# An encoder layer on one core: first front in half blocks, weight buffers, maxima and residual

## The chip, the core and the metric

The kernel runs on one core of one Trainium2 chip. It is measured in device microseconds for one execution, from start to end. The engines are named as in the profile: PE is TensorE (matrix products; PEld is its loading of weights), DVE is VectorE, ACT is ScalarE, POOL is GpSimd, SP is SyncE, which here only issues DMAs. Each engine works through its own instructions in the order in which they were laid down; a DMA issue is an instruction of the engine that issues it.

## The reference

One layer on 512 tokens of 2048 numbers, in float32. A layer norm; a projection whose columns split into a convolution group and a matrix-memory group (mLSTM, 8 heads); a mixing product and a second norm; then PEER: each token picks 8 x 16 of 16384 single-neuron experts by product keys, and the layer ends in a third norm.

```
def reference(x, ln_in_g, ln_in_b, w_in, b_gate, conv_w, conv_b, mh_norm_g, w_out,
              ln1_g, ln1_b, peer_wq, peer_keys, peer_u, peer_v, ln2_g, ln2_b):
    h = layernorm(x, ln_in_g, ln_in_b)
    for l in range(DEPTH):
        proj = h @ w_in[l]
        cB, cC, ch, q, k, v, o, gi, gf = jnp.split(proj, split_at, axis=-1)
        y_conv = cB * causal_dwconv(cC * ch, conv_w[l], conv_b[l])
...
        hm = mlstm_chunkwise(hd(q), hd(k), hd(v), logi, logf)
        hm = layernorm(hm, mh_norm_g[l].reshape(M_HEADS, M_HEAD_DIM),
...
        y_m = jax.nn.sigmoid(o) * hm.reshape(Bn, S, D_MLSTM)
        mix = jnp.concatenate([y_conv, y_m], axis=-1) @ w_out[l]
        h = layernorm(ALPHA * h + mix, ln1_g[l], ln1_b[l])
        ff = peer_ffn(h, peer_wq[l], peer_keys[l], peer_u[l], peer_v[l])
        h = layernorm(ALPHA * h + ff, ln2_g[l], ln2_b[l])
    return h

def peer_ffn(h, wq, keys, u, v):
...
        q = (xt @ wq).reshape(-1, PEER_HEADS, 2, PEER_HALF)
        s = jnp.einsum('thpc,hpnc->thpn', q, keys)
        sv, si = lax.top_k(s, PEER_TOPK)
...
        ue = jnp.take(u, eid, axis=0)
        act = jax.nn.gelu(jnp.einsum('thkd,td->thk', ue, xt).astype(jnp.float32), approximate=False)
        ve = jnp.take(v, eid, axis=0)
        return jnp.einsum('thk,thkd->td', (gate * act).astype(xt.dtype), ve)
```

## The kernel before

All weights arrive as **chunks** of 1 MB, tiles `raw` of 128 x 2048 numbers, 432 of them in the program. `load_split` (L90) issues the load on SP, and `split` (L81) cuts the chunk into two parts for three-pass products: ACT writes `hi`, the rounded value (L86), DVE writes `lo`, what is left (L87). `mm3` (L97 to L100) then makes three matmuls for each product: hi by hi (L98), with one low part (L99), with the other (L100). Which operand is the weight differs by stage; in the first front `lo` is read by L99, later by L100. `raw` has three buffers in the pool `wp`, `hi` and `lo` two each. A new `hi` waits until PE has finished the chunk that had its buffer before, and a new load waits until DVE has written the `lo` of the chunk three before.

The program goes through five parts.

- **First front** (`rows_block`, L311): the first 128 tokens go through the whole layer up to the choice of their experts, so that fetching can start early. It reads 56 chunks of the input projection (with `heads0`, `conv0` and the norms of the later tokens, `ln_later`, between them), 16 of the mixing product and 16 of the PEER query. A chunk is 12 matmuls of 512 columns.
- **Projections** of the other 384 tokens: `v_half` (8 chunks), then `head(h)` and `conv_block` (48 chunks), run in turns, three yields each (L660). A chunk is 48 matmuls of 384 columns. `head` makes q, k and the output gate; loads the head's stabilising maxima, `bM` (L611, one buffer), on SP; makes the weights W from them on ACT (L626, L623) and DVE (L622, L624), and the score tiles PJ (L631). After the first yield come the numerators (L641) and on DVE the denominators and statistics (L643 to L649); after the second the normalised rows `hm` (L655), which PE transposes (L656).
- **Mixing** (L673): 16 chunks of `w_out`, 36 matmuls of 512 columns each. `mix_out` (L683) fetches a piece of the residual, `hr` (L686, one buffer, issued by ACT), and adds it on DVE (L687). Then the norm, transposes (`to_t`) and the first query chunks.
- **Selection** (L744): the other queries, the top-16 choices, 32 hidden chunks (`u_chunk`, L735), and the weights of the chosen experts, spread into tables on PE and DVE (`build`, L803; its matmuls are L821, its table `wg`), which are written to DRAM as `w_d`.
- **Last stage** (L873): hidden chunks and value chunks (`v_part`, L913) for 320 tokens, 48 matmuls of 320 columns each; `make_g` (L897) multiplies a hidden chunk by a piece `wt` of the table, read back from `w_d` (L893). `AHEAD + MORE` hidden chunks, 32 + 3, are made before the loop and kept in DRAM.

Beside all this the first 128 tokens and half of the next 128 get their experts by **fetched rows** (`gather`, L507): POOL fetches 128 rows into a tile `gt`, and DVE multiplies them (L519 for u, L532 for v). These jobs are handed out by `advance`: `RATE_PROJ` = 1.5 for each chunk of projections and mixing, `RATE_MID` = 0.8 for each of the 32 hidden chunks, and the rest evenly over the last stage. `gt` has two buffers until the last stage and three in it (`gpool2`), and `flush(len(turn_[0]) - 1)` puts the product of a row one fetch behind it, or two in the last stage.

The order on each engine is made by a scheduler when the program is built; `high_priority` around the split puts `hi` and `lo` ahead of other work.

Of the kernel before, what the change touches and what calls it, by code (L numbers as in the profile page):

```python
# [8 lines left out]
F32 = mybir.dt.float32  # L9
# [10 lines left out]
P = 128  # L20
# [18 lines left out]
MORE = 3  # L39
# [6 lines left out]
RATE_PROJ = 1.5  # L46
# [6 lines left out]
def tile_kernel(ctx: ExitStack, tc: tile.TileContext, x, lin_g, lin_b, w_rows, w_proj, w_v, w_gate, b_gate,  # L53
# [24 lines left out]
    def raw_tile():  # L78
        return wp.tile([P, 2048], F32, name="raw", bufs=3)

    def split(raw, hi=None, lo=None, prio=PRIO):  # L81
        with tc.high_priority(offset=prio):
            if hi is None:
                hi = wp.tile([P, 2048], F32R, name="hi")
                lo = wp.tile([P, 2048], F32R, name="lo")
            ACT.activation(hi, raw, AF.Copy)  # L86
            DVE.tensor_sub(lo, raw, hi.bitcast(F32))  # L87
        return hi, lo

    def load_split(src, hi=None, lo=None):  # L90
        raw = raw_tile()
        nc.sync.dma_start(raw, src)
        return split(raw, hi, lo)
# [35 lines left out]
    def stats_tile():  # L129
        return stat.tile([P, 4, 6], F32, name="st", bufs=6)  # L130
# [173 lines left out]
    f0 = ExitStack()  # L304
    fy = f0.enter_context(tc.tile_pool(name="fy", bufs=1))
# [5 lines left out]
    def rows_block(src, b, xT):  # L311
        ps = pacc.tile([P, S], F32, name="acc")
        for pc in range(4):
            w = load_split(src[b, pc])
            for k in range(4):
                kk = 4 * pc + k
                mm3(ps, [a[:, kk, :] for a in xT], [a[:, k * S:(k + 1) * S] for a in w], kk == 0, kk == KD - 1)
        return ps
# [174 lines left out]
    f0.close()  # L493


    gpools = [ctx.enter_context(tc.tile_pool(name="gpool", bufs=2, side="right"))]
    turn_ = ["AA"]
    count = [0]
# [8 lines left out]
    def gather(src, idx):  # L507
        gt = gpools["AB".index(turn_[0][count[0] % len(turn_[0])])].tile([P, D], F32, name="gt")
        count[0] += 1
        ins = nc.gpsimd.indirect_dma_start(out=gt, out_offset=None, in_=src,  # L510
                                           in_offset=bass.IndirectOffsetOnAxis(ap=idx, axis=0))
        if last_mm[0] is not None:
            tc.add_manual_dep(ins.ins, last_mm[0].ins.name, SCHED, reason="gathers keep pace with the products")
        return gt

    def slot_jobs(idx, gate, rows, n, scale):
        def u_slot(s):
# [3 lines left out]
            flush(len(turn_[0]) - 1)  # L521
# [6 lines left out]
        def v_slot(s):  # L528
# [4 lines left out]
            flush(0 if s == n - 1 else len(turn_[0]) - 1)  # L533
# [14 lines left out]
    with ExitStack() as p1:  # L548
# [50 lines left out]

        def head(h):  # L600
            pq = proj_chunk(w_proj[24 + h], hT)
# [8 lines left out]
            bM = w2.tile([P, NL], F32, name="bM", bufs=1)  # L610
            nc.sync.dma_start(bM, bass.AP(tensor=nM_d.tensor, offset=nM_d.offset + h * S + P, ap=[[0, P], [1, NL]]))  # L611
# [61 lines left out]
    with ExitStack() as p1b:  # L673
        big = p1b.enter_context(tc.tile_pool(name="big2", bufs=1))
        lnp = p1b.enter_context(tc.tile_pool(name="lnp2", bufs=1))
        w2 = p1b.enter_context(tc.tile_pool(name="w3", bufs=1))
# [3 lines left out]
        r = big.tile([P, LT, D], F32, name="r32")  # L680
        sts = [stats_tile() for _ in range(LT)]

        def mix_out(ps, t, db):  # L683
            ds_ = slice(db * S, (db + 1) * S)
            hr = w2.tile([P, S], F32, name="hr")
            nc.scalar.dma_start(hr, h_d[:, t, ds_])  # L686
            DVE.scalar_tensor_tensor(r[:, t, ds_], hr, ALPHA, ps, op0=OP.mult, op1=OP.add)  # L687
# [182 lines left out]
    gpools.append(ctx.enter_context(tc.tile_pool(name="gpool2", bufs=1, side="right")))  # L870
    turn_[0] = "AAB"

    with ExitStack() as p3:  # L873
        ap = p3.enter_context(tc.tile_pool(name="accp", bufs=1))
# [87 lines left out]
        for kind, n in order:  # L962
# [3 lines left out]
            else:  # L966
# [9 lines left out]
              else load_split(vb[124 + db]) for db in range(4)]  # L976
        accO = [gpools[0].tile([P, D], F32, name="gt"), gpools[0].tile([P, D], F32, name="gt"),
                gpools[1].tile([P, D], F32, name="gt")]
# [107 lines left out]
```

## Time and profile before

| | before |
|---|---|
| time, median of 3 runs (lowest to highest) | 3341.19 us (3338.57 to 3356.52) |
| time of the profiled execution | 3352.37 us |
| its span | 3350.6 us |
| PE busy | 3095.6 us, 92% |
| DVE busy | 2779.4 us, 83% |
| ACT busy | 1149.2 us, 34% |
| DMA traffic | 947.44 MB, mean 283 GB/s |
| mean granted PE clock | 0.967 |

The profiled execution lies 11.2 us above the median of the runs. A share of busy time is a mean over parts with different limits, so the rows below are read part by part. The first front lasts until about 400 us, the projections until 1012, mixing until 1215, the selection until 1720 and the last stage from there to the end. Times in rows are counted from the start of the span.

### The profile page before, as it was taken

To read this page: it belongs to the slowest core of one execution; us is meant where nothing else is said; L and a number is where in the kernel's file an instruction comes from. 1 tells how busy PE (TensorE), PEld (TensorE's weight loads), DVE (VectorE), ACT (ScalarE), POOL (GpSimd) and SP (SyncE) were. 2 spreads that over 40 slices of the span, in tenths; PEclk is the share of its full clock that TensorE was granted. 3 is DMA by queue.
4 is the path that set the end of the run, shared out by engine and by line. 5 is a ranking of instruction groups with operands and counts; after the bars stand their busy time and mean duration, and the time that the engine had idled before them with its cause. 6 is when DMAs were issued, how large, how long until landed. Compare 5 with 4: busy or idle time off the path is not lost. (4 is left out here: it accounts for less than half of the span.)

```text
span 3350.6 us, 46462 instructions
## 1 busy us (share of the span) xinstructions
PE 3095.6 (92%) x19047; PEld 2931.8 (87%) x19047; DVE 2779.4 (83%) x3835; ACT 1149.2 (34%) x1107; POOL 670.4 (20%) x400
## 2 busy tenths in 40 slices
PE   6886888888988899999969999999999999999997
PEld 4665668888987699999969999999999999999995
DVE  7876877676767769998859999898889888889888
ACT  5554423332332223333323333333333333333332
POOL 0000012212222100110102122323223322333222
PEclk9999999999999989999979999999999999999999
DMA  7787557666767623666659999999999999899983
GB/s 274 284 300 259 212 220 258 253 241 241 266 247 289 258 104 121 234 251 239 245 192 354 359 351 345 338 350 344 339 352 338 344 345 351 328 348 343 348 318 130
DMA packets 183383, 947.44 MB, mean 283 GB/s; under 512 B 16818, under 2 KB 70850, under 8 KB 74434
## 3 DMA queue, kind: packets, MB, share of 16 engines
q1 hardware_dynamic: 116000, 496.52, 41.0%
q0 software_dynamic: 55296, 402.68, 32.1%
q10 hardware_dynamic: 11874, 45.28, 3.6%
q8 instruction: 149, 2.44, 0.3%
q14 instruction: 64, 0.52, 0.0%
HBM read 906.61 MB, written 37.21 MB: 282 GB/s over the span
## 5 line engine op out<-in xcount | busy, mean ns | idle before, releaser
L86 ACT ACTIVATE hi<-raw 128x2048 fp32r<-128x2048 f32 x427 | 818.1, 1916 | 1447.5 <-PE ph L99 594.7
L87 DVE TENSOR_TENSOR lo<-raw,hi 128x2048 fp32r<-128x2048 f32 x427 | 976.1, 2287 | 123.5 <-ACT hi L86 117.1
L100 PE MATMUL ph<-tth,lo 128*128 128x320 f32 (+3 forms) x2336 | 733.1, 314 | 5.1 <-DVE lo L87 5.1
L98 PE MATMUL ph<-tth,hi 128*128 128x320 f32 (+3 forms) x2336 | 732.9, 314 | 3.9 <-ACT gl L741 3.9
L99 PE MATMUL ph<-ttl,hi 128*128 128x320 f32 (+3 forms) x2336 | 733.8, 314 | 0.0
L98 PE MATMUL po<-gh,hi 128*128 128x320 f32 x1984 | 612.7, 309 | 21.0 <-ACT gh L909 18.3
L99 PE MATMUL po<-glo,hi 128*128 128x320 f32 x1984 | 613.1, 309 | 3.3 <-DVE glo L910 3.2
L100 PE MATMUL po<-gh,lo 128*128 128x320 f32 x1984 | 612.7, 309 | 3.5 <-DVE lo L87 3.5
L510 POOL DMA_INDIRECT gt<-in_u_dram,idx x192 | 319.0, 1661 | 1331.4 <-PE ph L99 419.9
L519 DVE SCALAR_TENSOR_TENSOR gt<-gt,rows 128x2048 f32<-128x2048 f32 x192 | 439.1, 2288 | 148.9 <-DMA gt<-in_u_dram,idx 148.5
L510 POOL DMA_INDIRECT gt<-in_v_dram,idx x192 | 328.7, 1712 | 795.7 <-PE po L99 278.6
L532 DVE SCALAR_TENSOR_TENSOR rows<-gt,wts,rows 128x2048 f32<-128x2048 f32 x192 | 450.6, 2347 | 27.5 <-DMA gt<-in_v_dram,idx 27.1
L100 PEld LDWEIGHTS ph<-tth,lo 128*128 128x128 f32 x2336 | 444.6, 190 | 6.9 <-DVE lo L87 6.9
L98 PEld LDWEIGHTS ph<-tth,hi 128*128 128x128 f32 x2336 | 444.6, 190 | 4.5 <-ACT gl L741 4.1
L99 PEld LDWEIGHTS ph<-ttl,hi 128*128 128x128 f32 x2336 | 444.6, 190 | 0.0
L98 PEld LDWEIGHTS po<-gh,hi 128*128 128x128 f32 x1984 | 372.4, 188 | 22.6 <-ACT gh L909 19.1
L99 PEld LDWEIGHTS po<-glo,hi 128*128 128x128 f32 x1984 | 372.5, 188 | 4.3 <-DVE glo L910 4.3
L100 PEld LDWEIGHTS po<-gh,lo 128*128 128x128 f32 x1984 | 372.6, 188 | 3.8 <-DVE lo L87 3.8
L923 DVE TENSOR_TENSOR accT<-accT,po 128x320 f32<-128x320 f32 x480 | 218.8, 482 | 79.2 <-PE po L100 71.9
L100 PE MATMUL acc<-tth,lo 128*128 128x384 f32 x768 | 267.2, 348 | 9.6 <-DVE lo L87 9.6
L98 PE MATMUL acc<-tth,hi 128*128 128x384 f32 x768 | 267.2, 348 | 0.0
L99 PE MATMUL acc<-ttl,hi 128*128 128x384 f32 x768 | 265.1, 345 | 0.0
(303 smaller groups left out, 3447.1 us busy)
## 6 DMA issues: line engine op xcount, KB each, us to landing
raw<-in_ut_dram SPq DMA_DIRECT2D x128, 1024.0 KB
raw<-in_vb_dram SPq DMA_DIRECT2D x128, 1024.0 KB
raw<-in_w_rows_dram SPq DMA_DIRECT2D x56, 1024.0 KB
raw<-in_w_proj_dram SPq DMA_DIRECT2D x48, 1024.0 KB
raw<-in_w_out_dram SPq DMA_DIRECT2D x32, 1024.0 KB
w_d<-wg ACTq DMA_DIRECT2D x10, 2048.0 KB
wt<-w_d SPq DMA_DIRECT2D x32, 640.0 KB
raw<-in_w_qrows_dram SPq DMA_DIRECT2D x16, 1024.0 KB
```

Of the source, the lines that this page charges most:

```text
L86: ACT.activation(hi, raw, AF.Copy)
L87: DVE.tensor_sub(lo, raw, hi.bitcast(F32))
L98: last_mm[0] = PE.matmul(ps, a[0], b[0], start=start, stop=False)
L99: PE.matmul(ps, a[0], b[1], start=False, stop=False)
L100: PE.matmul(ps, a[1], b[0], start=False, stop=stop)
L510: ins = nc.gpsimd.indirect_dma_start(out=gt, out_offset=None, in_=src, in_offset=bass.IndirectOffsetOnAxis(ap=idx, axis=0))
L519: pend.append(lambda: DVE.scalar_tensor_tensor(gt, gt, 1.0, rows(), op0=OP.mult, op1=OP.mult, accum_out=dots[:, s:s + 1]))
L532: pend.append(lambda: DVE.scalar_tensor_tensor(rows(), gt, wts[:, s:s + 1], rows(), op0=OP.mult, op1=OP.add))
L923: DVE.tensor_add(accT[:, dt_, :], accT[:, dt_, :], ps)
```

## The change

In the first front each chunk is split in two halves of 1024 columns: `load_split(..., parts=2)` issues hi, lo, hi, lo instead of hi, lo. Elsewhere the split is as before.

The third `raw` buffer no longer belongs to `wp`. It stands in a pool of its own, `wp0` during the first front and `wp1` in the last stage; between them (projections, mixing, selection) there are two. In exchange `gt` has three buffers throughout, and the product of a fetched row stands two fetches behind it throughout (`flush(2)`).

The maxima `bM` have two buffers and are loaded one head ahead, the first before the first head. The residual is loaded into `r` itself by three DMAs of 1 MB on SP, and `mix_out` adds onto it in place, so the twelve pieces `hr` on ACT's queue go. `MORE` is 4 instead of 3, `RATE_PROJ` 1.6 instead of 1.5.

```diff
-MORE = 3
+MORE = 4
...
-RATE_PROJ = 1.5
+RATE_PROJ = 1.6
...
     def raw_tile():
-        return wp.tile([P, 2048], F32, name="raw", bufs=3)
...
+        rawn[0] += 1
+        pool = more[-1] if more and rawn[0] % 3 == 0 else wp
+        return pool.tile([P, 2048], F32, name="raw")
...
+    def load_split(src, hi=None, lo=None, parts=1):
+        raw = raw_tile()
+        nc.sync.dma_start(raw, src)
+        with tc.high_priority(offset=PRIO):
             if hi is None:
                 hi = wp.tile([P, 2048], F32R, name="hi")
                 lo = wp.tile([P, 2048], F32R, name="lo")
-            ACT.activation(hi, raw, AF.Copy)
-            DVE.tensor_sub(lo, raw, hi.bitcast(F32))
+            n = 2048 // parts
+            for i in range(parts):
+                c = slice(i * n, (i + 1) * n)
+                ACT.activation(hi[:, c], raw[:, c], AF.Copy)
+                DVE.tensor_sub(lo[:, c], raw[:, c], hi[:, c].bitcast(F32))
         return hi, lo
...
     f0 = ExitStack()
+    more.append(f0.enter_context(tc.tile_pool(name="wp0", bufs=1)))
...
-            w = load_split(src[b, pc])
+            w = load_split(src[b, pc], parts=2)
...
     f0.close()
-    gpools = [ctx.enter_context(tc.tile_pool(name="gpool", bufs=2, side="right"))]
-    turn_ = ["AA"]
+    more.clear()
+    gpool = ctx.enter_context(tc.tile_pool(name="gpool", bufs=3, side="right"))
...
-            flush(len(turn_[0]) - 1)
+            flush(2)
...
+        def load_bM(h):
+            bM = w2.tile([P, NL], F32, name="bM", bufs=2)
+            nc.sync.dma_start(bM, bass.AP(tensor=nM_d.tensor, offset=nM_d.offset + h * S + P, ap=[[0, P], [1, NL]]))
+            return bM
+
+        bMs = [load_bM(0)]
+
         def head(h):
+            if h + 1 < NH:
+                bMs.append(load_bM(h + 1))
+            bM = bMs[h]
...
-            bM = w2.tile([P, NL], F32, name="bM", bufs=1)
-            nc.sync.dma_start(bM, bass.AP(tensor=nM_d.tensor, offset=nM_d.offset + h * S + P, ap=[[0, P], [1, NL]]))
...
         r = big.tile([P, LT, D], F32, name="r32")
+        for t in range(LT):
+            nc.sync.dma_start(r[:, t, :], h_d[:, t, :])
...
-            hr = w2.tile([P, S], F32, name="hr")
-            nc.scalar.dma_start(hr, h_d[:, t, ds_])
-            DVE.scalar_tensor_tensor(r[:, t, ds_], hr, ALPHA, ps, op0=OP.mult, op1=OP.add)
+            DVE.scalar_tensor_tensor(r[:, t, ds_], r[:, t, ds_], ALPHA, ps, op0=OP.mult, op1=OP.add)
...
-    gpools.append(ctx.enter_context(tc.tile_pool(name="gpool2", bufs=1, side="right")))
-    turn_[0] = "AAB"
     with ExitStack() as p3:
+        more.append(p3.enter_context(tc.tile_pool(name="wp1", bufs=1)))
```

The scheduler lays the work out anew. Three places where the order moves follow, first of the kernel before, then of the changed one; the line numbers of each are its own.

DVE in the mixing product of the first front, around the sum with the residual of the second column block (L458 before, L464 after); `lo` with a number is one chunk's low part. Before:

```order
L87 TENSOR_TENSOR lo_1852<-raw_1849,hi_1851 128x2048
L87 TENSOR_TENSOR lo_1873<-raw_1870,hi_1872 128x2048
L458 SCALAR_TENSOR_TENSOR rows0_82<-rows0_82,acc_1794 128x512
L459 BN_STATS st_1718<-rows0_82 128x6
L87 TENSOR_TENSOR lo_1891<-raw_1888,hi_1890 128x2048
```

After:

```order
L97 TENSOR_TENSOR lo_1981<-raw_1978,hi_1980 128x1024 x2
L97 TENSOR_TENSOR lo_2004<-raw_2001,hi_2003 128x1024
L464 SCALAR_TENSOR_TENSOR rows0_82<-rows0_82,acc_1917 128x512
L97 TENSOR_TENSOR lo_2004<-raw_2001,hi_2003 128x1024
L465 BN_STATS st_1833<-rows0_82 128x6
L97 TENSOR_TENSOR lo_2024<-raw_2021,hi_2023 128x1024 x2
```

Each chunk's low part is two instructions now, and other work of DVE can stand between the two.

DVE in a head of the projections, from the last score tiles PJ to the statistics. L519 and L523 are the product of a fetched row, L622 and L634 a first step of W from `bM`, L643 and L655 the first step of the denominators. Before:

```order
L631 TENSOR_TENSOR PJ_4761<-sm,W 128x256
L631 TENSOR_TENSOR PJ_4769<-sm,W 128x128
L622 TENSOR_SCALAR W<-bM,aT 128x128
L519 SCALAR_TENSOR_TENSOR gt,dots<-gt,rows_82 128x2048
L643 TENSOR_SCALAR dn<-sm,em 128x1
L87 TENSOR_TENSOR lo<-raw,hi 128x2048
L644 TENSOR_SCALAR dn<-sm,dn 128x1
```

After:

```order
L643 TENSOR_TENSOR PJ_4951<-sm,W 128x256
L643 TENSOR_TENSOR PJ_4959<-sm,W 128x128
L523 SCALAR_TENSOR_TENSOR gt,dots<-gt,rows_82 128x2048 x2
L97 TENSOR_TENSOR lo<-raw,hi 128x2048
L655 TENSOR_SCALAR dn<-sm,em 128x1 x2
L656 TENSOR_SCALAR dn<-sm,dn 128x1 x2
L657 RECIPROCAL dn<-dn 128x1
```

The step of the next head's W has left its place ahead of the denominators, and a second product of fetched rows and the low part stand there now.

PE where the last table is built and the last stage begins. `pw` is the table, `po` a value chunk, which needs the table, `ph` a hidden chunk, which doesn't. Before:

```order
L821 LDWEIGHTS ob_13460
L821 MATMUL pw<-oa,ob_13460 128x128
L98 MATMUL po<-gh,hi 128x320 x2
L99 MATMUL po<-glo,hi 128x320
L100 MATMUL po<-gh,lo 128x320
L98 MATMUL ph<-tth,hi 128x320
```

After:

```order
L832 LDWEIGHTS ob_13635
L832 MATMUL pw<-oa,ob_13635 128x128
L103 MATMUL ph<-tth,hi 128x320
L104 MATMUL ph<-ttl,hi 128x320
L105 MATMUL ph<-tth,lo 128x320
```

Behind the last table stood at once the first products that need it; now 144 matmuls of hidden chunks, three whole chunks, stand between them.

## Rows read from the trace of the kernel before

**Rows 1.** Busy time by stretch: stretch, us, each engine's, granted clock, DMA share, GB/s.

```profile
28.00:256.00 228.00, 186.72 (x811) 140.99 (x812) 181.35 (x219) 132.01 (x110) 0.00 (x0) 0.96 0.78 285
256.00:330.00 74.00, 55.20 (x214) 40.46 (x212) 48.83 (x32) 35.65 (x21) 0.00 (x0) 0.94 0.76 273
346.00:400.00 54.00, 42.97 (x189) 32.73 (x190) 47.92 (x119) 28.73 (x22) 0.00 (x0) 0.97 0.69 247
462.00:1012.00 550.00, 485.98 (x2646) 466.35 (x2644) 383.67 (x587) 171.56 (x206) 121.28 (x79) 0.94 0.68 250
1012.00:1215.00 203.00, 182.17 (x827) 153.83 (x828) 133.64 (x140) 44.36 (x38) 37.01 (x21) 0.88 0.64 237
1705.00:1753.00 48.00, 26.85 (x179) 24.36 (x178) 18.93 (x47) 10.55 (x19) 0.00 (x0) 0.64 0.57 185
1753.00:3235.00 1482.00, 1475.51 (x10043) 1473.21 (x10042) 1336.48 (x1244) 487.87 (x437) 437.12 (x255) 1.00 0.93 345
```

**Rows 2.** PE's waits, 0 to 400 us: who, for whom, us, times, longest.

```profile
PE acc L99 <- DVE lo L87: 57.5, 42, 3.5
```

**Rows 3.** Instruction groups, 0 to 400 us: busy us, mean ns, idle before, releaser.

```profile
L87 DVE TENSOR_TENSOR lo<-raw,hi 128x2048 fp32r<-128x2048 f32 x88 | 200.8, 2288 | 70.2 <-ACT hi L86 69.7
L86 ACT ACTIVATE hi<-raw 128x2048 fp32r<-128x2048 f32 x88 | 168.4, 1913 | 150.0 <-PE acc L100 129.4 <-DMA raw<-in_w_rows_dram 14.4 <-DVE rsa L110 2.5
...
L139 DVE TENSOR_TENSOR ttl<-sm,tth 128x512 fp32r<-128x512 f32 x12 | 7.8, 681 | 0.0
...
L138 ACT ACTIVATE tth<-sm 128x512 fp32r<-128x512 f32 x12 | 6.4, 594 | 0.0
```

**Rows 4.** ACT's timeline in the front's mixing product: start, us, instruction, idle before.

```profile
289.55 1.92 ACT L86 ACTIVATE hi<-raw 128x2048 fp32r<-128x2048 f32 x1 [2.46 <-PE acc L100]
...
296.72 1.91 ACT L86 ACTIVATE hi<-raw 128x2048 fp32r<-128x2048 f32 x1 [2.46 <-PE acc L100]
```

**Rows 5.** PE's timeline in the same stretch.

```profile
287.02 0.40 PE L100 MATMUL acc<-hi,y0l 128*128 128x512 f32 x1
287.25 0.39 PE L98 MATMUL acc<-hi,y0h 128*128 128x512 f32 x1
```

**Rows 6.** The chain of waits near the end: a weight load, issue to landing.

```profile
3283.39 4.97 DMA raw<-in_vb_dram
```

**Rows 7.** PE's waits, 462 to 1012 us.

```profile
PE sm L656 <- DVE hm L655: 39.8, 7, 7.9
PE acc L100 <- DVE lo L87: 9.6, 6, 3.4
```

**Rows 8.** DVE's timeline in one head of the projections.

```profile
607.87 0.29 DVE L622 TENSOR_SCALAR W<-bM,aT 128x128 f32<-128x128 f32 x1 [5.42 <-DMA bM<-nM_d]
...
620.16 2.29 DVE L519 SCALAR_TENSOR_TENSOR gt<-gt,rows 128x2048 f32<-128x2048 f32 x1 [1.95 <-DMA gt<-in_u_dram,idx]
...
626.30 0.34 DVE L655 TENSOR_SCALAR hm<-hm,hmv,hrs 128x128 f32<-128x128 f32 x1
```

**Rows 9.** Busy time by stretch, columns as in rows 1: just behind that head's stall.

```profile
626.70:633.50 6.80, 6.80 (x32) 6.63 (x33) 5.04 (x9) 1.92 (x1) 2.32 (x2) 0.77 0.44 154
```

**Rows 10.** PE's waits, 1012 to 1215 us.

```profile
PE acc L99 <- DVE lo L87: 12.1, 3, 6.7
```

**Rows 11.** ACT's timeline in the mixing part.

```profile
1135.02 1.92 ACT L86 ACTIVATE hi<-raw 128x2048 fp32r<-128x2048 f32 x1 [10.85 <-DVE r L687]
```

**Rows 12.** PE's waits, 1190 to 1745 us.

```profile
PE po L98 <- ACT gh L909: 18.3, 1, 18.3
```

**Rows 13.** The chain of waits at the start of the last stage.

```profile
1720.64 11.77 DMA w_d<-wg
...
1732.46 4.59 DMA wt<-w_d
```

**Rows 14.** ACT's timeline in the projections: the splits of successive chunks.

```profile
706.60 1.92 ACT L86 ACTIVATE hi<-raw 128x2048 fp32r<-128x2048 f32 x1 [6.40 <-PE acc L99]
714.92 1.92 ACT L86 ACTIVATE hi<-raw 128x2048 fp32r<-128x2048 f32 x1 [6.03 <-PE acc L99]
```

More of the change, by code (lines that the diff above doesn't have):

```diff
@@ L78, in raw_tile @@
     def raw_tile():
-        return wp.tile([P, 2048], F32, name="raw", bufs=3)
-    def split(raw, hi=None, lo=None, prio=PRIO):
-        with tc.high_priority(offset=prio):
+        rawn[0] += 1
+        pool = more[-1] if more and rawn[0] % 3 == 0 else wp
+        return pool.tile([P, 2048], F32, name="raw")
+    rawn = [0]
+    more = []
+    def load_split(src, hi=None, lo=None, parts=1):
+        raw = raw_tile()
+        nc.sync.dma_start(raw, src)
+        with tc.high_priority(offset=PRIO):
             if hi is None:
@@ L85, in split @@
                 lo = wp.tile([P, 2048], F32R, name="lo")
-            ACT.activation(hi, raw, AF.Copy)
-            DVE.tensor_sub(lo, raw, hi.bitcast(F32))
+            n = 2048 // parts
[3 more added lines that the diff above has]
+                DVE.tensor_sub(lo[:, c], raw[:, c], hi[:, c].bitcast(F32))
         return hi, lo
[L90 to L93, printed above, removed]
     last_mm = [None]
@@ L493, in tile_kernel @@
     f0.close()
-    gpools = [ctx.enter_context(tc.tile_pool(name="gpool", bufs=2, side="right"))]
-    turn_ = ["AA"]
-    count = [0]
+    more.clear()
+    gpool = ctx.enter_context(tc.tile_pool(name="gpool", bufs=3, side="right"))
     pend = []
@@ L507, in gather @@
     def gather(src, idx):
-        gt = gpools["AB".index(turn_[0][count[0] % len(turn_[0])])].tile([P, D], F32, name="gt")
-        count[0] += 1
+        gt = gpool.tile([P, D], F32, name="gt")
         ins = nc.gpsimd.indirect_dma_start(out=gt, out_offset=None, in_=src,
@@ L532, in v_slot @@
             pend.append(lambda: DVE.scalar_tensor_tensor(rows(), gt, wts[:, s:s + 1], rows(), op0=OP.mult, op1=OP.add))
-            flush(0 if s == n - 1 else len(turn_[0]) - 1)
+            flush(0 if s == n - 1 else 2)
         return ([lambda s=s: u_slot(s) for s in range(n)] + [act_job]
@@ L675, in tile_kernel @@
         lnp = p1b.enter_context(tc.tile_pool(name="lnp2", bufs=1))
-        w2 = p1b.enter_context(tc.tile_pool(name="w3", bufs=1))
         psm = p1b.enter_context(tc.tile_pool(name="psm2", bufs=2, space=PSUM))
@@ L976, in tile_kernel @@
               else load_split(vb[124 + db]) for db in range(4)]
-        accO = [gpools[0].tile([P, D], F32, name="gt"), gpools[0].tile([P, D], F32, name="gt"),
-                gpools[1].tile([P, D], F32, name="gt")]
+        accO = [gpool.tile([P, D], F32, name="gt") for _ in range(LT)]
         for t, (c0, m) in enumerate(TGRP):
```

## The prediction

> **What bounds the kernel now.** I read the stretches first [rows 1], then the waits of PE part by part [rows 2, 7, 10, 12], because PE is busy 92% of the span and a gain must come out of its idle time or its clock. Three parts differ. From 1753 to 3235 us PE works 1475.5 of 1482 us at granted clock 1.00: nothing that frees another engine can shorten this. In the first front PE works 186.7 of 228 us, 55.2 of 74 and 43.0 of 54, and one cause names most of the rest: it waits 57.5 us, 42 times, for a low part from DVE [rows 2]. In the projections it works 486 of 550, with 39.8 us in seven waits for `hm` and 9.6 for `lo` [rows 7]. Mixing and the start of the last stage run at mean clocks of 0.88 and 0.64, and PE waits 18.3 us in one piece for the first `gh` [rows 12].
>
> **The first front in halves.** Two successive splits of ACT start 7.17 us apart (289.55, 296.72), and the gap between them ends with PE (2.46 us after L100) [rows 4]: `hi` has two buffers, so this is the time of two chunks. Matmuls of 512 columns start 0.23 apart [rows 5], so PE has 24 x 0.233 = 5.60 us of work in it. The 7.17 is a chain that goes round: hi 1.91 + lo 2.29 [rows 3, 4] + 11 matmuls (2.57) + some 0.4 of handing over. In halves the second hi half can run beside the first lo half. No row has such an instruction of 1024 columns; 512 columns take ACT 0.594 us and DVE 0.681 against 1.913 and 2.288 for 2048 [rows 3], so 1024 take by a straight line 1.03 and 1.22. The chain becomes 1.03 + 1.22 + 2.57 + 0.4 = 5.22 us, less than PE's 5.60, so PE would set the pace: 1.57 us a pair. The price is 2 x 1.22 - 2.29 = 0.15 us of DVE a chunk and 0.15 of ACT; ACT is idle 150 us in front of these splits [rows 3], so only DVE's counts.
> From 28 to 256 us (56 chunks) 28 pairs x 1.57 = 44, but DVE has 181.4 of work there [rows 1], with the halves 181.4 + 56 x 0.15 = 189.8: no more than 38 can go. Between the low parts DVE has convolution, heads and norms that come in their own order, so I let it be 93% busy: 189.8 / 0.93 = 204, a gain of 24. From 256 to 330 DVE is busy 48.8 of 74: 8 pairs x 1.57 = 12.6, less the first and last pair's edges, 11. From 346 to 400 DVE is busy 47.9 of 54 and gets 2.4 more: 2. The rest of the front is norm and transposes in sequence and stays. **Sum 37**, bounds 15 (DVE at 90% in the first stretch, as in the last stage's 1336 of 1482, gives 17, and a little loss at the end) and 58 (all of the wait).
>
> **The maxima a head ahead.** In the head at 600 to 627 us DVE's L622 waits 5.42 us for `bM` till 607.87 [rows 8]. That is W of the next head, yet behind it in DVE's order stand a fetched row's product and the denominators of this head. Then a product waits 1.95 for its row and takes 2.29 (620.16), and `hm` comes at 626.30. PE stalls 7.9 for it [rows 7]. The new order has no L622 there, but a second product and a low part: two products, lo, then the denominators. I take away the 5.42 and the 1.95 (the product stands two fetches behind its row now) and add part of a product that moved in: hm some 6.0 earlier, three quarters of the stall, and by that share of the 39.8 us 0.7 x 39.8 = 28. Of the waits for `lo` (9.6) I take 6, since DVE's waits for rows stood in front of those too. Behind the stall the clock is 0.77 over 6.8 us [rows 9], a mean of its two levels (1.2 and 2.4 GHz), PE having idled before; that costs 0.23 x 6.8 = 1.6 a stall, 7 x 1.6 = 11, of which 9 goes with them. **Sum 43**, bounds 15 (the second product keeps DVE as late in most heads, and only the longest stalls shrink) and 75 (all waits, 49, 11 of clock, and half again of the loss that the mean of 0.94 over 550 us shows, 33).
> `RATE_PROJ` 1.6 puts about 7 more products here, 16 us of DVE; DVE is busy 384 of 550, so 0, and as many leave the last stage, which PE sets: 0.
>
> **The residual.** In mixing ACT's split waits 10.85 us behind the sum on DVE [rows 11]: ACT stands at its own issue of `hr`, whose one buffer is still being read, and the splits are queued behind it. PE feels this as 12.1 us for `lo` [rows 10]. With `r` loaded ahead, ACT has only splits: 10 of the 12.1 goes, and 2 of clock. Against this the three loads of 1 MB go on SP's queue between the weights. A chunk is 36 matmuls, 8.4 us; the third one has 16.8 us until PE needs it and then three more loads of 4.97 [rows 6], 14.9, before it: about even, so I take 2 for them. **Sum 10**, bounds 0 (SP's loads wait for buffers and PE for the first weights) and 20.
> What moves here is the queue, not the bytes. The Trainium skill ("DMA: Bandwidth & Descriptors", section "Issuing engines are not separate DMA queues") says that all issuing engines feed the same 16 DMA engines, and that issuing from several only saves the sequencer's time for the issue, usually little beside the transfer. By that rule alone this term would be 0 and my sum 99. I go by the row: the 10.85 us is an issue that stands in order on ACT and waits for a buffer.
>
> **The start of the last stage.** The last table is written from 1720.64 for 11.77 us, read back in 4.59 [rows 13], and PE waits 18.3 [rows 12]. Now 144 matmuls of hidden chunks stand in between. 10043 matmuls in 1482 us [rows 1] are 0.148 each: 21 us of work that has to be done anyway and was done later. It covers the 18.3; their weights are fetched beside a DMA share of 0.57. PE also comes out of the gap at full clock, 1 us or so. **Sum 19**, bounds 10 (the hidden chunks wait for loads that share the DMA with the table) and 26 (18.3 and 8 of the half clock around it).
>
> **Two raw buffers between the parts.** `raw` is freed when lo is done, hi 1.92 + lo 2.29 = 4.2 us after its split starts. In the projections splits start 8.32 us apart [rows 14], so with two buffers a load must land 16.64 - 4.2 = 12.4 us after its issue; it takes 4.97 where the trace shows one alone [rows 6]. DMA share is 0.64 to 0.68 there. I take 0. `MORE` moves one chunk out of the loop and adds none: 0.
>
> **The sum.** 37 + 43 + 10 + 19 = 109. The profiled execution, 3352.4, would become 3243. It lies 11.2 above the median, so from the median 3341.2 - 109 = **3232**.
>
> **Rivals.**
> *The stalls only move on DVE.* DVE takes its work in order; if the two products that now stand ahead of the denominators wait for their rows, hm comes hardly earlier (projections 15), and if DVE in the front runs lo's halves behind its other work, 18 remains of 37; mixing 8, start 15: 56 in all, **3285**. For it: the new order has two products of 2.29 where one stood. Against: 7.4 us of waiting were in front of that hm.
> *The halves don't let PE start early.* If the order or the waits let PE take the low matmuls only after the whole part, the pair's chain is 1.03 + 2 x 1.22 + 2.57 + 0.4 = 6.44, 0.73 instead of 1.57 a pair: 44 pairs x 0.73 = 32 at most, by the same limits 20. Sum 92, **3249**. For it: lo's halves need not stand together, as the order of DVE shows, where a sum stands between two of them.
> *Two raw buffers starve PE: slower.* 120 chunks (56 of the projections, 16 of mixing, 48 of queries and hidden chunks) have two buffers. A load that takes over 12.4 us makes PE wait the excess once for two chunks, 60 times. It cancels the gain from 109 / 60 = 1.8 us of excess on, so from loads of 14.2 us; at 15 the price is 60 x 2.6 = 156, **3388**. For it: three fetches in flight instead of two, which compete with the loads, and 237 to 250 GB/s that can go up to 345 [rows 1]. Against: 14.2 is nearly three times 4.97.
> *Nothing to be measured.* If the scheduler's new order gives back elsewhere what the waits lose: **3341**. Against: four separate places would have to fail.
>
> **How the numbers follow.** Forecast 0.76 (with sizes that vary), stalls that move 0.10, whole low parts 0.05, starved 0.05, nothing 0.04. About 0.5% (17 us) is what a measurement of this kernel can tell from no change. Faster: 0.76 + 0.10 + 0.05 = 0.91, less 0.01 for a weak second case: 0.90; the same 0.05, slower 0.05. Lower ends sum to 15 + 15 + 0 + 10 = 40 (3301), upper ends to 58 + 75 + 20 + 26 = 179 (3162). That all four meet their upper ends is less likely than that all are small, for then one late DVE is enough; so I take the low sum whole and 167 of the high one: 3174 to 3301. What is left out is the two last cases and some 0.1 of the first.
>
> **What would show it.** In the changed kernel's profile: PE's waits for lo in the front fall from 57.5 to under 25, and the pair of splits from 7.17 to about 5.6; if it stays over 6.4, the whole low part is awaited. PE's waits for hm fall from 39.8 to about 12, and no DVE wait for `bM` is left. ACT's waits behind the sum with r are gone in mixing. The 18.3 before the first value chunk becomes 0 to 3, with hidden chunks in its place. From there on the rate per matmul stays 0.148. I am wrong if ACT's splits wait for `raw` loads by more than a few us in projections or selection (two buffers too few), if PE waits for hm as long as before under another releaser (DVE waiting for rows), or if the front's DVE is at 95% and PE still waits 40.

## The result and the profile after

The changed kernel takes 3209.93 us (median of 4 runs, 3204.9 to 3218.8) beside 3344.43 us for the kernel before (4 runs, 3338.57 to 3356.52): a ratio of 0.9596, interval 0.9561 to 0.9632. That is 134.5 us less; 109 were forecast, to 3232, in a range of 3174 to 3301. The two profiled executions lie 133.6 us apart (spans 3350.6 and 3217.0), so the stretches of the two traces add up to the change.

To see where, both are cut at the same work: the start of ACT's split of the same chunk. Busy time by stretch of the changed kernel (start and end, length, then each engine's busy time, PE's clock, DMA share and GB/s, as in [rows 1]):

```profile
18.20:221.20 203.00, 184.34 (x839) 141.36 (x839) 184.81 (x264) 141.26 (x168) 0.00 (x0) 0.99 0.86 311
221.20:286.40 65.20, 53.04 (x218) 39.42 (x218) 50.11 (x60) 35.75 (x40) 0.00 (x0) 0.92 0.87 320
286.40:350.10 63.70, 52.58 (x244) 42.47 (x244) 55.81 (x102) 38.85 (x46) 0.00 (x0) 0.92 0.74 262
350.10:879.80 529.70, 514.04 (x2858) 488.54 (x2858) 448.25 (x771) 186.58 (x210) 151.02 (x87) 0.99 0.79 287
879.80:1031.00 151.20, 139.40 (x594) 114.09 (x593) 115.41 (x120) 38.32 (x34) 40.37 (x22) 0.94 0.80 307
1031.00:1513.00 482.00, 472.37 (x3166) 458.00 (x3165) 425.58 (x1086) 164.51 (x191) 48.17 (x24) 0.98 0.55 196
1513.00:1640.10 127.10, 104.29 (x722) 97.33 (x721) 85.75 (x165) 41.28 (x61) 6.64 (x4) 0.77 0.63 224
```

The kernel before, the three of these stretches that the text needs in full (first front's first 56 chunks, projections, start of the last stage):

```profile
17.60:258.20 240.60, 194.66 (x859) 148.03 (x860) 191.69 (x231) 139.16 (x116) 0.00 (x0) 0.96 0.77 280
400.90:1002.30 601.40, 535.03 (x2861) 503.48 (x2860) 428.44 (x706) 183.69 (x210) 126.22 (x83) 0.94 0.67 245
1653.40:1775.70 122.30, 96.31 (x686) 90.94 (x685) 79.86 (x158) 41.83 (x64) 9.10 (x5) 0.82 0.65 227
```

| stretch (same chunks) | before, us | after, us | change | forecast |
|---|---|---|---|---|
| first front, 56 chunks | 240.6 | 203.0 | -37.6 | -24 |
| its mixing and query, 32 chunks | 142.7 | 128.9 | -13.8 | -13 |
| projections, 56 chunks | 601.4 | 529.7 | -71.7 | -43 |
| mixing, 16 chunks | 161.1 | 151.2 | -9.9 | -10 |
| selection | 490.0 | 482.0 | -8.0 | 0 |
| start of the last stage | 122.3 | 127.1 | +4.8 | -19 |
| from there to the end | 1574.9 | 1576.9 | +2.0 | 0 |

So the sum hides two steps that came out otherwise: the projections gave far more, and the start of the last stage nothing. The selection hands 36 table matmuls on to that start (its count falls from 3202 to 3166); the two together are 3.2 us shorter.

Each kernel here has one trace, and the same work differs between traces: in the ten kernels of this text whose first front has halves, the first stretch takes 201.2 to 208.7 us. A few us of any row can be this.

**First front.** From 0 to 350 us: PE's waits for `lo`, against 57.5 in [rows 2], and the groups of the halves on DVE and on ACT, with what they wait for, against [rows 3]:

```profile
PE acc L104 <- DVE lo L97: 11.7, 22, 1.5
L97 DVE TENSOR_TENSOR lo<-raw,hi 128x1024 fp32r<-128x1024 f32 x176 | 207.2, 1220 | 32.4 <-ACT hi L96 32.0
L96 ACT ACTIVATE hi<-raw 128x1024 fp32r<-128x1024 f32 x176 | 176.7, 1054 | 95.2 <-PE acc L105 44.2 <-DMA raw<-in_w_rows_dram 25.6 <-DMA raw<-in_w_out_dram 13.8
```

A half takes DVE 1.220 us and ACT 1.054 (1.22 and 1.03 were forecast). The new late thing is in the third row: ACT waits 25.6 + 13.8 us for loads, where [rows 3] had 14.4. ACT's timeline in the front's mixing product, as in [rows 4], shows it; each row is the two halves of a chunk:

```profile
251.24 2.01 ACT L96 ACTIVATE hi<-raw 128x1024 fp32r<-128x1024 f32 x2 [0.79 <-PE acc L105]
...
257.27 2.02 ACT L96 ACTIVATE hi<-raw 128x1024 fp32r<-128x1024 f32 x2 [0.77 <-DMA raw<-in_w_out_dram]
...
263.11 2.01 ACT L96 ACTIVATE hi<-raw 128x1024 fp32r<-128x1024 f32 x2 [0.61 <-DMA raw<-in_w_out_dram]
```

A pair takes 6.03 and 5.84 us instead of 7.17; PE's own 5.60 isn't reached, because the weights now come too late. Whether the three `raw` buffers hold them back or the rate of the DMA is not shown: its share is 0.87 here at 320 GB/s, and the last stage ran at 0.93 and 345 [rows 1].

**Projections.** From 350.1 to 879.8 us, two of PE's waits (that for `hm` was 39.8 in [rows 7]) and DVE's for fetched rows:

```profile
PE sm L653 <- DVE PJ L643: 4.4, 2, 3.9
PE sm L668 <- DVE hm L667: 1.1, 1, 1.1
DVE gt L523 <- DMA gt<-in_u_dram,idx: 55.6, 33, 4.6
```

In the kernel before, from 400.9 to 1002.3 us, this last row read as follows, and DVE waited for the maxima as well, which it doesn't now:

```profile
DVE gt L519 <- DMA gt<-in_u_dram,idx: 103.8, 44, 4.9
DVE W L622 <- DMA bM<-nM_d: 31.8, 6, 6.8
```

The head that [rows 8] showed, in DVE's timeline after:

```profile
594.54 2.29 DVE L523 SCALAR_TENSOR_TENSOR gt<-gt,rows 128x2048 f32<-128x2048 f32 x1
...
596.75 2.29 DVE L523 SCALAR_TENSOR_TENSOR gt<-gt,rows 128x2048 f32<-128x2048 f32 x1
...
598.97 2.29 DVE L97 TENSOR_TENSOR lo<-raw,hi 128x2048 fp32r<-128x2048 f32 x1
601.17 0.34 DVE L655 TENSOR_SCALAR dn<-sm,em 128x1 f32<-128x1 f32 x2
```

Both products that stand ahead of the denominators start with no idle time before them: their rows had landed. Of the seven stalls of PE for `hm` one of 1.1 us is left, and with them goes the half clock behind them (mean 0.94 before, 0.99 after).

**Start of the last stage.** The 18.3 us of [rows 12] are gone too, but PE waits elsewhere now (1560 to 1640 us):

```profile
PE ph L103 <- ACT gl L752: 9.2, 1, 9.2
PE ph L103 <- ACT hi L96: 4.7, 1, 4.7
...
PE ph L105 <- DVE lo L97: 1.4, 1, 1.4
```

ACT's timeline there says why:

```profile
1580.23 1.91 ACT L96 ACTIVATE hi<-raw 128x2048 fp32r<-128x2048 f32 x1 [2.07 <-DMA gl<-hs_d]
...
1601.36 1.28 ACT L918 ACTIVATE gh<-gl 128x320 fp32r<-128x320 f32 x3 [5.69 <-DVE gl L914]
1602.57 0.90 ACT L752 ACTIVATE gl<-ph 128x320 f32<-128x320 f32 x2
```

The gelu of two finished hidden chunks (L752) stands on ACT behind `gh` (L918), which waits for the table. `gl`, the tile of a finished hidden chunk, has four buffers, and `make_g(0)` to `make_g(3)`, written ahead of the hidden chunks, hold all four until the table is there. So of the three chunks that were to cover the wait two run, and PE waits 9.2 us before the third, as it waited for `gh` before.

### The profile page after: what moved, and what is told of

It is laid out like the page before. It is cut to its first block, busy times and chain, and to the rows that moved or that the text cites. A ratio compares the mean times of both kernels' runs of the same rounds, so it can differ in the third digit from the quotient of the medians.

```text
span 3217.0 us, 46592 instructions
## 1 busy us (share of the span) xinstructions
PE 3066.1 (95%) x19047; PEld 2913.5 (91%) x19047; DVE 2783.2 (87%) x3923; ACT 1160.0 (36%) x1195; POOL 686.2 (21%) x400
## 4 chain that ended last, share of the span: by engine, by line
PE 44%; DVE 4%; DMA 1%; issue 1%; ACT 0%; DVEq 0%; SPq 0%; ACTq 0%
PE po L103 8%; PE po L104 8%; PE po L105 8%; PE ph L105 7%; PE ph L103 7%; PE ph L104 7%; DVE lo L97 1%; DVE rows L536 1%; DVE accT L932 0%; DVE gt L936 0%; DMA gt<-in_v_dram,idx 0%; DMA fold<-rows 0%; DMA wt<-w_d 0%; DMA w_d<-wg 0%; DVE st L1013 0%
## 5 line engine op out<-in xcount | busy, mean ns | idle before, releaser
L96 ACT ACTIVATE hi<-raw 128x2048 fp32r<-128x2048 f32 (+1 forms) x515 | 827.2, 1623 | 1427.8 <-PE ph L104 604.3
L97 DVE TENSOR_TENSOR lo<-raw,hi 128x2048 fp32r<-128x2048 f32 (+1 forms) x515 | 983.0, 1923 | 113.5 <-ACT hi L96 110.1
L514 POOL DMA_INDIRECT gt<-in_u_dram,idx x192 | 347.3, 1809 | 1049.4 <-PE acc L104 262.4
L514 POOL DMA_INDIRECT gt<-in_v_dram,idx x192 | 318.0, 1656 | 973.3 <-PE po L104 411.4
L523 DVE SCALAR_TENSOR_TENSOR gt<-gt,rows 128x2048 f32<-128x2048 f32 x192 | 437.9, 2288 | 87.3 <-DMA gt<-in_u_dram,idx 86.9
L536 DVE SCALAR_TENSOR_TENSOR rows<-gt,wts,rows 128x2048 f32<-128x2048 f32 x192 | 450.8, 2348 | 18.0 <-DMA gt<-in_v_dram,idx 17.6
L105 PE MATMUL acc<-tth,lo 128*128 128x384 f32 x768 | 258.7, 337 | 5.1 <-DVE lo L97 5.1
L103 PE MATMUL acc<-tth,hi 128*128 128x384 f32 x768 | 259.3, 338 | 0.0
L104 PE MATMUL acc<-ttl,hi 128*128 128x384 f32 x768 | 257.6, 335 | 0.0
```

Of the source, the lines that this page charges most:

```text
L96: ACT.activation(hi[:, c], raw[:, c], AF.Copy)
L97: DVE.tensor_sub(lo[:, c], raw[:, c], hi[:, c].bitcast(F32))
L103: last_mm[0] = PE.matmul(ps, a[0], b[0], start=start, stop=False)
L104: PE.matmul(ps, a[0], b[1], start=False, stop=False)
L105: PE.matmul(ps, a[1], b[0], start=False, stop=stop)
L523: pend.append(lambda: DVE.scalar_tensor_tensor(gt, gt, 1.0, rows(), op0=OP.mult, op1=OP.mult, accum_out=dots[:, s:s + 1]))
```

## Experiments

Each is the changed kernel with one edit, or the kernel before with one edit; only the last two add theirs to the version in front of them. "Changed" is 3209.9; "before" is the kernel before, measured again beside each group of runs (medians 3336 to 3345). Where the difference of the medians and the ratio say something different, both are given.

### The front's halves: taken away, and alone

```diff
-            w = load_split(src[b, pc], parts=2)
+            w = load_split(src[b, pc])
```

> The changed kernel with the chunks of the first front split whole again; all else stays. Theory (the chain of a pair of chunks, hi, lo, 11 matmuls, sets the front): the pair of splits goes back from about 5.6 to 7.17 us, PE's waits for lo in the front from 11.7 to about 57, and the time rises by most of the front's 50.8 us, to 3250 to 3262. Rival (the front gained by the new order or by its third buffer): within 8 us of 3210.

3251.05 us (3243.94 to 3255.59), 41 above changed. PE's waits for `lo`, 17 to 400 us, and then ACT's splits at the same place of the front:

```profile
PE acc L104 <- DVE lo L97: 57.7, 45, 3.9
```

```profile
289.45 1.91 ACT L96 ACTIVATE hi<-raw 128x2048 fp32r<-128x2048 f32 x1 [2.45 <-PE acc L105]
...
296.62 1.92 ACT L96 ACTIVATE hi<-raw 128x2048 fp32r<-128x2048 f32 x1 [2.46 <-PE acc L105]
```

The pair is back at 7.17, the waits at 57.7: the chain is what it was read to be. The front itself ends 50.5 us later; in the 32 chunks behind it 8.4 of that is caught up again.

The other way round, the kernel before with the halves alone (the same `parts=2`):

> The kernel before with the halves of the first front alone. Theory: all of the front's 50.8 us: 3344 - 50 = 3294 (3285 to 3302), the rest of the program as before. Rival (the front needs the other edits too, or later stages give it back): 3310 to 3344.

3303.88 us beside 3337.7; ratio 0.9893 (0.9845 to 0.9941): 34 us by the medians, 36 by the ratio, so between theory and rival. In its trace the front ends 47.7 us earlier and 13.6 are given back over the next 32 chunks, where DVE waits 73.7 us for rows (50.8 in the kernel before). The front's gain is its own, but of its 50 us only 34 to 41 arrive at the end.

### The maxima: late again, and ahead alone

```diff
-        bMs = [load_bM(0)]
...
-            if h + 1 < NH:
-                bMs.append(load_bM(h + 1))
-            bM = bMs[h]
...
             ACT.activation(sg, po_, AF.Sigmoid)
+            bM = load_bM(h)
```

(and one buffer instead of two)

> The changed kernel with one buffer for the maxima, loaded in the head itself as before. Theory (late maxima hold DVE's queue in front of the denominators): of the 71.6 us that the projections gained, 28 to 50 go, with PE's waits for hm back above 20 us: 3238 to 3260. Rival (the gain is that of the products, which stand two fetches behind their row): 3210 to 3220.

3204.79 us (3199.3 to 3209.2), ratio to before 0.9574 (0.9521 to 0.9627): no difference from the changed kernel that stands clear of its runs. So the theory's time doesn't come. But neither does the wait that it is about: in the projections the late load is waited for by ACT.

```profile
ACT W L634 <- DMA bM<-nM_d: 20.7, 6, 6.3
...
DVE gt L523 <- DMA gt<-in_u_dram,idx: 50.0, 33, 3.9
```

PE's waits have no row for `hm` at all, and DVE's none for the maxima, against 31.8 us before the change. The order on DVE says why. In the kernel before, the first step of the next head's W stands ahead of this head's denominators for six of the seven heads that follow another; here for none. It comes behind their first steps, mostly behind the statistics too, where this head hardly waits for it. So the run shows that a late load is harmless in this order, and not what the wait on DVE had cost.

Then the kernel before with the maxima ahead alone:

> The kernel before with the maxima in two buffers, a head ahead, alone. Theory (they carry most of the projections' 71.6 us): PE's waits for hm fall from 43 to under 20 and the time by 28 to 50 us: 3294 to 3316. Rival (the product of the row that stands there waits for its fetch then, and hm is as late): 3330 to 3344.

3321.04 us (10 runs) beside 3337.7; ratio 0.9944 (0.9926 to 0.9962): 17 us by the medians, 19 by the ratio. Between theory and rival: DVE's wait for the maxima is gone, PE's waits for `hm` fall from 39.8 to 21.8, and DVE waits for rows nearly as long as before:

```profile
PE sm L664 <- DVE hm L663: 21.8, 7, 5.8
DVE gt L519 <- DMA gt<-in_u_dram,idx: 94.3, 49, 5.7
```

So in the kernel before the maxima were behind nearly half of PE's waits for `hm`, and the rows are the likely cause of the other half; the next runs take them up.

### The exchange of buffers: taken away, and alone

```diff
-        pool = more[-1] if more and rawn[0] % 3 == 0 else wp
-        return pool.tile([P, 2048], F32, name="raw")
+        return wp.tile([P, 2048], F32, name="raw", bufs=3)
...
-            flush(2)
+            flush(len(turn_[0]) - 1)
```

(and two buffers of `gt`, a third in the last stage, as before)

> The changed kernel with three weight buffers throughout and two buffers for fetched rows until the last stage, their product one fetch behind. Theory (the third row buffer takes away half of DVE's waits for rows in the projections, 103.8 to 55.6 us, and a part of PE's waits hangs on them): 3225 to 3245. Rival 1 (only the maxima counted): 3205 to 3215. Rival 2 (two weight buffers cost time somewhere): below 3205.

3302.79 us (3292.75 to 3304.37), 93 above changed: far above what theory and rivals said, and more than the whole gain of projections and mixing (82). Its projections take 600.1 us for the same 56 chunks, with these waits:

```profile
PE sm L652 <- DVE PJ L642: 22.1, 12, 6.8
PE sm L667 <- DVE hm L666: 16.4, 7, 4.2
...
DVE gt L522 <- DMA gt<-in_u_dram,idx: 123.2, 47, 6.0
```

DVE has no wait for the maxima in this kernel, as in the changed one, so the 93 us are not theirs. That named the exchange as the cause, and the next run tried it alone on the kernel before:

> The kernel before with the exchange of buffers alone: two weight buffers between the parts, three for fetched rows throughout, their product two fetches behind; maxima, residual, whole chunks and rates as before. New theory (after the run without it rose to 3303 and the one with late maxima stayed at 3205, the exchange carries the projections): PE's waits for hm and the scores nearly go, DVE's waits for rows halve, and the time falls by 60 to 90 us: 3250 to 3280. Rival (the exchange counts only with the higher rate of fetches and the free queue of ACT; alone it is worth what the maxima alone were): 3310 to 3330.

3254.3 us (3249.31 to 3258.71) beside 3345.07; ratio 0.9719 (0.9658 to 0.9779): 91 us by the medians, 94 by the ratio, as the theory said. Its projections take 518.5 us, less than the 529.7 of the changed kernel, with the maxima and ACT's queue of before (and the lower rate of fetches, 1.5):

```profile
DVE gt L523 <- DMA gt<-in_u_dram,idx: 41.0, 28, 3.5
...
PE sm L660 <- DVE hm L659: 0.3, 1, 0.3
```

DVE's wait for the maxima is gone here too, though they are loaded late: in this order too W's first step stands behind the denominators, as in the run with late maxima, and ACT waits 29.9 us for the load. So the gains of the two edits made alone can overlap and must not be added.

### The place of the product, or the buffer

```diff
-            flush(2)
+            flush(1)
```

> The changed kernel with all its buffers, but the product of a fetched row one fetch behind it in the program instead of two. Theory (it is the place of the product in DVE's order that counts: DVE stands before a row that is still under way, with all its other work behind it): DVE's waits for rows in the projections go back above 90 us and the time rises to 3270 to 3300. Rival (it is the buffer: fetches start earlier, whatever the order of the products): 3205 to 3230.

3327.4 us (10 runs), even further up than expected, but the stretches say where: the projections lose only 24.5 us (529.7 to 554.2) and mixing nothing, while the last stage loses 87, from the first value chunks on. The first row is of DVE in the projections; the other two are of the last stage, DVE's wait and PE's:

```profile
DVE gt L523 <- DMA gt<-in_u_dram,idx: 81.7, 43, 4.6
```

```profile
DVE rows L536 <- DMA gt<-in_v_dram,idx: 169.3, 93, 6.6
...
PE ph L105 <- DVE lo L97: 48.6, 23, 4.5
```

In the changed kernel the same wait of L536 is 17.6 us in the last stage. So in the projections the place of the product is worth 24.5 of the 70 us that the whole exchange is worth there, and the buffer the rest (neither theory alone was right). In the last stage the place decides; but there the product stood two fetches behind before the change as well, so these 87 us are no part of the gain. The mechanism is one: DVE works in order, and a product that stands before its row has landed holds back the next chunk's `lo` (48.6 us of PE's waiting above).

### The residual on ACT's queue again

```diff
-        for t in range(LT):
-            nc.sync.dma_start(r[:, t, :], h_d[:, t, :])
...
+            hr = w2.tile([P, S], F32, name="hr")
+            nc.scalar.dma_start(hr, h_d[:, t, ds_])
-            DVE.scalar_tensor_tensor(r[:, t, ds_], r[:, t, ds_], ALPHA, ps, op0=OP.mult, op1=OP.add)
+            DVE.scalar_tensor_tensor(r[:, t, ds_], hr, ALPHA, ps, op0=OP.mult, op1=OP.add)
```

> The changed kernel with the residual in pieces on ACT's queue again. Theory (ACT stands behind its own issue): ACT's waits behind the sum with r come back, to about 50 us, PE's wait for lo in mixing to about 12, and the time rises by about 10 us: 3217 to 3225. Rival (which queue issues does not count, as the Trainium skill's page DMA: Bandwidth & Descriptors, section Issuing engines are not separate DMA queues, has it): within 4 us of 3210.

3220.82 us (3213.86 to 3230.57), 11 above changed, but the intervals overlap (0.9564 to 0.9676 against 0.9561 to 0.9632) and the mixing stretch of its trace is only 1.8 us longer. ACT's waits there:

```profile
ACT hi L96 <- DVE r L699: 21.3, 2, 11.1
```

The wait behind ACT's own issue is back, as the mechanism says, at 21 us and not 50; that it costs PE 10 is not shown. Among the traces of this text with two weight buffers in mixing it takes 145.5 to 153.0 us where the residual is loaded ahead, and 153.0 and 144.9 in the two with the pieces. By the rule that the expectation names the difference would be nothing, and this run can't contradict it.

### Weight buffers: the price of one

```diff
-        pool = more[-1] if more and rawn[0] % 3 == 0 else wp
-        return pool.tile([P, 2048], F32, name="raw")
+        pool = more[-1] if more and rawn[0] % 3 else wp
+        return pool.tile([P, 2048], F32, name="raw", bufs=2 if pool is not wp else 1)
```

> The changed kernel with one weight buffer between the parts instead of two (three in the first front and the last stage as now). It prices the rival that two buffers starve PE. With one buffer a chunk takes a load and its split one after the other: 4.97 + 4.2 = 9.2 us where the load is alone, and loads beside fetches took up to 10 us, so up to 14. PE needs 8.3 us a chunk in projections and mixing (72 chunks) and 7.1 in the 48 others. Theory (buffers times PE's time for a chunk against load plus split decides): at least 72 x 0.9 + 48 x 2.1 = 165 us, with loads of 7 us in the mean 72 x 2.9 + 48 x 4.1 = 405: 3375 to 3615, and ACT's waits for raw become its longest. Rival (the copies hi and lo, two buffers each, hide most of it): below 3300.

3369.2 us (3 runs), 159 above changed, and 1.05% above the kernel before (ratio 1.0052 to 1.0158): just under the lower end of the theory, which is the sum with undisturbed loads (165). By stretch the two don't agree. The traces add 74 us in the projections, 28 in mixing and 50 from there to the first value chunk; the lower end has 50, 14 and 101. So the near total is in part two errors that cancel. ACT's waits, 350 to 1050 us:

```profile
ACT hi L96 <- DMA raw<-in_w_proj_dram: 217.0, 38, 11.9
```

With two buffers the same wait is 4.1 us, once, in the projections. So one buffer starves PE and two don't; the rule that priced it holds for the total only. The loads that the rival with two buffers needed, over 12.4 us one after the other, didn't come: with the exchange alone those of the projections land in 4.8 to 9.4 us.

### The start of the last stage

```diff
+        for c in range(AHEAD, AHEAD + MORE):
+            nc.scalar.dma_start(hs_d[c], u_chunk(c, g2, GL))
         for k in range(4):
             make_g(k)
-        for c in range(AHEAD, AHEAD + MORE):
-            nc.scalar.dma_start(hs_d[c], u_chunk(c, g2, GL))
```

> The changed kernel with the four hidden chunks of the last stage's start written ahead of the first four products with the table, instead of behind them. Theory (the ring of four gl, all held by products that wait for the table, and ACT's order keep the third hidden chunk back, so PE waits 9.2 us): that wait goes, 8 to 12 us: 3198 to 3204. Rival (the table's way through DRAM is the bound there, and PE waits for the first gh behind the hidden chunks instead): 3207 to 3213.

3211.8 us (3210.02 to 3213.21): what the rival said. The 9.2 us wait shrinks to 2.2, and PE stands 5.1 before the first value chunk instead; this stretch of its trace is 0.1 us longer than that of the changed kernel. PE's waits, 1560 to 1640 us:

```profile
PE po L103 <- ACT gh L918: 5.1, 1, 5.1
PE ph L103 <- ACT hi L96: 4.6, 1, 4.6
...
PE ph L103 <- ACT gl L752: 2.2, 1, 2.2
```

With that, and the count of weight buffers started anew:

```diff
         more.append(p3.enter_context(tc.tile_pool(name="wp1", bufs=1)))
+        rawn[0] = 0
```

> The kernel before this one, and the count of weight buffers started anew at the last stage, so that its first two loads need no memory of the selection. Theory (the first hidden chunk's load waits for the selection's tables, and ACT's split of it holds back the next ones and the last write of the table): PE's 4.7 and 1.4 us go too, and half a clock with them: another 5 to 9 us, 3190 to 3198. Rival (the clock stays down from the table's small products, and the loads are late anyway): within 3 us of the kernel before this one.

3206.58 us (3192.96 to 3213.86): between theory and rival, and not apart from the changed kernel. The stretch is 6.6 us shorter; the 4.6 for hi is gone, and 6.9 us for `gl` stand in its place.

What both left is in front of the waits. PE's timeline in the second of them and, below it, the changed kernel's busy time in the same piece of work:

```profile
1547.90 1.58 PE L832 MATMUL pw<-oa,ob 128*128 128x128 bf16 x12 [0.42 <-DVE ob L825]
1549.90 1.59 PE L832 MATMUL pw<-oa,ob 128*128 128x128 bf16 x12 [0.42 <-DVE ob L825]
```

```profile
1541.90:1577.50 35.60, 28.40 (x216) 23.41 (x216) 31.64 (x86) 10.50 (x18) 0.00 (x0) 0.50 0.31 125
```

Table matmuls stand in a row here, a group of 12 every 2.00 us as DVE makes their operands, and PE runs at 0.50 of its clock; the stretch of the changed kernel holds 216 of them. The whole row without hidden chunks is 192 matmuls long in the kernel before, 252 in the changed one (five groups, 10 us, more) and 204 in the second version. Between the first and the last of the 960 table matmuls there are 24 hidden chunks now and 26 before. So, by this count, of the three chunks that now stand behind the tables two were taken from among them, where they had filled PE while DVE made operands. The next run is the second version with work taken from DVE there:

```diff
-RATE_MID = 0.8
+RATE_MID = 0.4
```

> The kernel with the hidden chunks first and the weight buffers counted anew, with 0.4 instead of 0.8 fetched rows for each hidden chunk of the selection, the others moving to the last stage. Theory (DVE, not PE, sets the selection's end: 204 to 252 small matmuls of the last tables stand in a row at one group of 12 in 2 us, at half the clock, and the hidden chunks that could fill PE there are used up): with some 13 products of 2.3 us less on DVE the row of tables shrinks to 11 matmuls and 15 to 30 us go: 3178 to 3192. Rival (what leaves DVE there comes back in the last stage, where DVE is busy 0.9 of the time): 3202 to 3215.

3192.26 us (3189.19 to 3204.33), at the upper edge of the theory; all four runs lie below the lowest of the changed kernel (3204.9). The ratio to before is 0.9538 (0.9476 to 0.9601). That is 18 us below the changed kernel in the median, though the two intervals overlap, and 14 below the version it was made from, whose runs it overlaps. The longest row of table matmuls is 25 now. The stretch from the selection's last queries to the last stage's first value chunks, here and then in the changed kernel, with the same matmuls:

```profile
1192.00:1607.70 415.70, 404.64 (x2904) 394.58 (x2903) 339.69 (x689) 154.01 (x192) 26.62 (x16) 0.99 0.61 220
```

```profile
1202.00:1640.10 438.10, 409.10 (x2903) 394.53 (x2902) 367.67 (x707) 155.66 (x193) 53.62 (x27) 0.93 0.66 237
```

22.4 us go, of which the 24 chunks behind it give back 7.8.

## Why the prediction was right, and where it was not

- **What bounds the kernel**: right. From the first value chunk to the end the time moved by 2 us, and all the gain lies in the parts in which PE waited.
- **The first front in halves**: the chain, the sizes of the halves and the mechanism held; taking the edit away brought the 7.17 back. The step that was mis-sized is the first stretch, 24 forecast and 37.6 measured. PE's idle time there falls from 45.9 to 18.7 us, 27; most of the rest is the granted clock, 0.96 to 0.99, which is 0.04 x 240.6 less 0.01 x 203, some 8 us, and the working had no clock in it. The step that failed beside it is "PE would set the pace": the loads do, at 5.84 to 6.03 a pair. The working asked neither how soon the three buffers come free nor how fast the DMA can fill them. And 8 to 14 of the 50 are given back behind the front.
- **The maxima a head ahead**: the sign was right, the cause about half of it. The row with the longest wait in front of `hm` (5.42 us for `bM`) was read as the cause, the 1.95 for the row as a detail. With the maxima in time and nothing else, 17 to 19 us go and PE still waits 21.8 us for `hm`, so the step "I take away the 5.42 and the 1.95" gave to the maxima what was mostly the rows'. It also took the early load for what moves W's step out of the denominators' way, but with the exchange the order moves it with the load as late as before. The 103.8 us of DVE's waits for rows were the better witness: many short waits that each set all of DVE back.
- **Two raw buffers between the parts**: "I take 0" was right for the weights, but the other side of the exchange had no term of its own: 91 to 94 us alone, more than four fifths of the whole forecast. That the total came near is in part luck: 43 for the maxima stood for it. Mixing has two buffers as well, and there ACT waits 20 us for loads, and PE 4.2 for ACT's split in this trace.
- **The residual**: 10 forecast, 9.9 measured in the stretch, but the run without it doesn't say that the residual did it, and the exchange alone gave mixing 16 us. That the number was met is luck as far as is known.
- **The start of the last stage**: wrong. 18.3 us went and 9.2 + 4.7 + 1.4 of new waits and more half clock came. "Work that has to be done anyway and was done later" was the step that failed; two of the three chunks came from among the tables, where they had covered DVE's pace. The ring of four `gl` could have been read in the code.
- **Rivals**: that stalls only move came true in that one place alone. Starvation didn't come, and the run with one buffer bears out its price in the total only. `RATE_PROJ` and `MORE` were not tried alone.

## What to carry to other kernels

On an engine that works in order, a short wait for a fetch costs all that is queued behind it: sum the many short waits before the single long one, and put the consumer of a fetch as many turns behind it as there are buffers to let it. When work is moved to cover a wait, find out from where; if it covered something there, and what holds its buffers here, the wait only moves. Undo an edit and make it alone, and look whether the wait that should come back did: undoing the early load gave 0 and making it alone some 18 us, because the order had moved its reader in the meantime.

## What the runs showed of the hardware that was not expected

The same 985 matmuls (the first query chunks of the selection and the transposes ahead of them) took 171.0 us in the changed kernel and 162.1 in the one with late maxima. The rows of both, changed first, with the piece in which they differ below it:

```profile
1031.00:1202.00 171.00, 167.56 (x985) 160.81 (x984) 143.66 (x544) 50.13 (x59) 1.19 (x1) 0.94 0.33 112
1043.60:1064.10 20.50, 20.50 (x97) 20.13 (x96) 5.96 (x10) 1.34 (x3) 0.00 (x0) 0.50 0.18 75
```

```profile
1019.60:1181.70 162.10, 157.90 (x985) 151.30 (x984) 143.36 (x543) 49.97 (x59) 1.19 (x1) 1.00 0.35 118
```

In the one, 20.5 us from 1043.6 on run at half clock, with PE busy all through; in the 12.6 us before them the clock was 1.00 and PE busy for 10.9. In the other the clock never falls. The kernel before has such a piece there as well (1176 to 1203). Of the fourteen kernels of this text, the one with a single weight buffer aside, five take 171.0 to 172.3 us here at a clock of 0.92 to 0.94, and eight 161.8 to 162.9 at 0.99 to 1.00. The edits don't part them: kernels with two and with three weight buffers here stand in both groups. With one trace for each kernel it stays open whether the kernel or the execution decides; some 9 us of a difference between two traces can be this alone.
